# A hybrid decoder layer: every third weight piece with seven products instead of every fourth, and two of the four weight sums formed by accumulating transfers

## The chip, the core and the metric

The kernel runs on one core of one Trainium2 chip. The metric is device time in microseconds (us) of one execution; lower is better. TensorE (PE) does the matmuls, VectorE (DVE) and ScalarE (ACT) the elementwise work, SyncE (SP) issues most transfers, and GpSimd (POOL) does almost nothing before the change.

## The reference

One layer in float32, with 256 tokens, 16 meta tokens ahead of them and a width of 2048:

```python
h = RMSNorm(x)
[B, C, v | z, xBC, dt] = h @ W_in            # 2048 x 12320
yA = GroupRMSNorm(B * conv3(C * v))
yB = GroupRMSNorm(SSD(conv4(xBC), dt) * silu(z))
x = x + RMSNorm([yA | yB] @ W_out)           # 4096 x 2048
x = x + RMSNorm(relu(RMSNorm(x) @ W1)^2 @ W2)  # 2048 x 8192, 8192 x 2048
```

The change touches the two products whose result has the tokens on the partitions: `@ W_out` and `@ W2`.

## The kernel before

**Split products.** Every float32 operand is split into a high part in a shorter format (a cast on ScalarE) and a low part (a subtraction on VectorE). A product is then three matmuls: high by high, high by low, low by high. For a weight piece the parts are `wh` and `wl`, for activations `jh` and `jl`.

**Pieces.** All weights are read once, in pieces of 1 MB, in an order written out in the list `pieces`. `load(i)` gets a raw buffer (`raw`, 3 buffers), issues the transfer on SyncE's queue, and splits it into `wh` (3 buffers) and `wl` (2 and an extra one for every third piece). Program order is by hand: while piece i is multiplied, pieces up to i + 2 are loaded. The order on each engine's queue is laid out at compile time by a planner that simulates the engines with its own costs; each engine then runs its queue in order.

**The two stages.** `tok_stationary` does `W_out` (16 pieces a half) and `W2` (32 a half). The output's 2048 columns are done in two halves h of 1024. A piece holds 256 rows (two blocks of 128, index k) by 1024 columns (two blocks of 512, index nb); the tokens are two blocks of 128 (blk). A plain piece is 2 x 2 x 2 products of 128 x 128 by 128 x 512, added up in the four PSUM banks `four` (one for each blk and nb): 24 matmuls (L786 to L788).

**Seven-product pieces.** For the pieces listed in `fast`, the 2 x 2 x 2 block product is done with seven products in place of eight, in the manner of Strassen and Winograd: 21 matmuls (L817 to L819). It takes four mixed left blocks (`js`, split into `mix`, L772 to L777) and four mixed weight blocks `t` (L189 to L191), split into `th` and `tl`. Three products go to banks of `four`, four to the other banks, `shared`, which collect the terms that several results have in common. After the last such piece of a half, `spread_shared` (L829 to L834) forms from them one addend for each result, in SBUF. At the end of the half `leave` adds each addend to its bank (L848), squares and sums for the norm (L906), and multiplies by the gain (L853, L861). For the very last bank of the second half the addend is split by `shared_last` and added through TensorE with two matmuls by the identity (L842). The tiles `t`, `th` and `tl` have one buffer each.

**Order around it.** `add_up(i + 3)` asks for a seven-product piece's raw and forms its sums three pieces ahead, before `load` splits its `wh` and `wl`. `W_out` has `fast` pieces 7 and 10 in the first half, 2, 6 and 10 in the second; `W2` has every fourth from 4 to 28, and from 2 to 26. At the end of `W_out`, `residual` (L956) and transposes (L965) turn the first 128 tokens for the feed-forward stage. `dt_consts` (L477 on) copies constants from `cst_sb` at the start, where SyncE issues alternate between input rows and weights.

```python
halve(raw, wh, wl, slice(1, 2))                   # load(), a seven-product piece
nc.scalar.copy(wh[:, 0, :512], raw[:, 0, :512])
nc.vector.tensor_sub(wl[:, 0, :512], raw[:, 0, :512], wh[:, 0, :512])   # L206
```

Of the kernel before, what the change touches and what calls it, by code (L numbers as in the profile page):

```python
# [9 lines left out]
F32 = mybir.dt.float32  # L10
F32R = mybir.dt.float32r
# [35 lines left out]
def hymba_layer(ctx: ExitStack, tc: tile.TileContext, ht, x, meta, vec, cst, g1, g3,  # L47
# [131 lines left out]

    seven, sums = {}, {}  # L180

    def add_up(i):

        if i not in seven or i in sums:
            return
        raw = fetch(i, ("raw",))[0]
        rows_in(i, raw, slice(0, 2))
        t, th, tl = seven[i]()
        nc.vector.tensor_sub(t[:, 0:2], raw[:, :, 512:], raw[:, 0].rearrange("p (a n) -> p a n", a=2))  # L189
        nc.vector.tensor_sub(t[:, 2], raw[:, 1, 512:], t[:, 0])  # L190
        nc.vector.tensor_sub(t[:, 3], raw[:, 1, :512], t[:, 2])  # L191
        for half in (slice(0, 2), slice(2, 4)):
            halve(t, th, tl, half)
        sums[i] = (raw, th, tl)

    def load(i):
# [3 lines left out]
        if i in seven:  # L200
            add_up(i)
            raw, th, tl = sums[i]
            wh, wl = fetch(i, ("wh", "wl"))
            halve(raw, wh, wl, slice(1, 2))
# [6 lines left out]
        for k in range(0, nk, 1 if ff1 else nk // 2):  # L211
            if ff1:
                g = vcol(V_G2 + (i - base_ff1) % 4 * 4 + k)
                act(wh[:, k], raw[:, k], AF.Copy, scale=g)  # L214
                stt(wl[:, k], raw[:, k], g, wh[:, k].bitcast(F32), op0=ALU.mult, op1=ALU.subtract)  # L215
            else:
                halve(raw, wh, wl, slice(k, k + nk // 2))
# [9 lines left out]
    cst_sb = const.tile([P, NCST], F32, name="cst_sb")  # L227
# [69 lines left out]
    with ExitStack() as p1:  # L297
# [25 lines left out]
        def split_input(k):  # L323
# [9 lines left out]
            if k == 8:  # L333
                nc.sync.dma_start(vec_sb[:, V_GCN:], vec[:, V_GCN:])
                nc.sync.dma_start(cst_sb, cst)

        first = []

# [136 lines left out]
        def dt_consts():  # L475
            ts(vec_sb[:, V_CW:V_DSK], vec_sb[:, V_CW:V_DSK], 0.5, None, op0=ALU.mult)
            nc.vector.tensor_copy(nsel.rearrange("p i m -> p (i m)"), cst_sb[:, C_NS:C_NS + 384])  # L477
# [266 lines left out]
    def tok_stationary(base, korder, src, parity, dst, gain, ssq, r, tail, done, between, late=None, sixth=None,  # L744
# [12 lines left out]
        def prep(i):  # L757
# [10 lines left out]
            if base + i in seven:  # L768
# [3 lines left out]
                nc.vector.tensor_add(a[:, 0], a21, a22)  # L772
                nc.vector.tensor_sub(a[:, 1], a[:, 0], a11)
                nc.vector.tensor_sub(a[:, 2], a11, a21)
                nc.vector.tensor_sub(a[:, 3], a12, a[:, 1])
# [49 lines left out]
        def spread_shared(x, h):  # L825
# [7 lines left out]
            add(e12, e12, e22)  # L833
            add(e22, e21, e22)  # L834

        def shared_last(o):

            hi = jit.tile([P, 2, SEQ], F32R, tag="jh", name="sh").rearrange("p a b -> p (a b)")
            lo = jit.tile([P, 2, SEQ], F32R, tag="jl", name="sl").rearrange("p a b -> p (a b)")
            nc.scalar.copy(hi, part(1, 1, 1))  # L840
            nc.vector.tensor_sub(lo, part(1, 1, 1), hi)
            later(3, lambda: [mm(o, lhsT=idr, rhs=e, start=False, stop=False) for e in (hi, lo)])  # L842

        def leave(o, h, blk, nb):
            i = 2 * h + nb
            ns = slice(512 * i, 512 * (i + 1))
            if fast[h] and (h, blk, nb) != (1, 1, 1):
# [316 lines left out]
```

## Time and profile before

| | |
|---|---|
| median of 3 runs | 1514.04 us (1513.62 to 1514.47) |
| the profiled execution's own time | 1515.25 us |
| its span, first to last instruction | 1513.5 us |
| granted TensorE clock, mean | 0.995 |
| busy: PE, PEld, DVE, ACT, POOL | 1491.7, 1338.3, 1123.7, 839.8, 1.1 us |
| HBM read | 277.90 MB, 185 GB/s over the span |

The profile shows one execution. A row of a timeline is start, duration, engine, line, operation, output<-inputs, count; in square brackets stands how long the engine was idle before it and what it waited for. Rows of groups give the busy time, the mean duration of one in ns, and the idle time before. PEld is the loading of a matmul's stationary operand, which overlaps matmuls; a matmul's duration includes its pipeline, so its cost in a full queue is the distance from one start to the next. An elementwise operation's duration likewise overlaps its neighbours' by some 0.08 us.

### The profile page before, as it was taken

Reading aid. Unit: us, or ns where it says so; the run is one execution under the profiler, and the core shown is the slowest. Engines: PE = TensorE matmul, PEld = TensorE weight load, DVE = VectorE, ACT = ScalarE, POOL = GpSimd, SP = SyncE. Lnnn points to the kernel's source line nnn. Section 1 sums busy time; section 2 is a strip of 40 time slices with the busy share of each in tenths; the row PEclk is TensorE's granted clock in tenths of the full one; section 3 lists DMA queues with packets and bytes.
Section 4 is the critical chain, followed back from the end, with each engine's and each line's share of the span. In section 5 each row is a group of like instructions: output and inputs, shape, how many; then the busy total and the mean of one; then the engine's idle time right before and its main releaser. Section 6 shows DMA issues by size and latency. Waiting matters only on the chain.

```text
span 1513.5 us, 23117 instructions
## 1 busy us (share of the span) xinstructions
PE 1491.7 (99%) x9183; PEld 1338.3 (88%) x9183; DVE 1123.7 (74%) x1774; ACT 839.8 (55%) x1301; POOL 1.1 (0%) x8
## 2 busy tenths in 40 slices
PE   8999999999999999999999999999999999999997
PEld 8999899999999999988877888888888888888885
DVE  7698888667866776798878666566666788789875
ACT  6655555455545554555556656555556556566562
POOL 0000000000000000000000000000000000000000
PEclk9999999999999999999999999999999999999998
DMA  9665554556455656575653555565556565656652
GB/s 306 230 190 166 142 152 155 167 174 173 156 165 170 169 165 211 183 247 177 213 195 139 180 187 190 195 193 184 189 189 204 197 198 195 219 172 233 197 195 82
DMA packets 151677, 281.50 MB, mean 186 GB/s; under 512 B 8064, under 2 KB 59392, under 8 KB 150912
## 3 DMA queue, kind: packets, MB, share of 16 engines
q1 hardware_dynamic: 150848, 275.83, 56.8%
q10 hardware_dynamic: 720, 4.19, 0.7%
q8 instruction: 72, 1.18, 0.3%
q14 instruction: 37, 0.30, 0.1%
HBM read 277.90 MB, written 2.10 MB: 185 GB/s over the span
## 4 chain that ended last, share of the span: by engine, by line
PE 95%; DMA 2%; DVE 1%; ACT 1%; SPq 0%; issue 0%; DVEq 0%; ACTq 0%
PE mm L1083 15%; PE mm L643 11%; PE mm L642 10%; PE mm L641 10%; PE mm L787 9%; PE mm L788 9%; PE mm L786 9%; PE mm L1084 7%; PE mm L638 3%; PE mm L819 2%; PE mm L818 2%; PE mm L817 2%; DMA raw<-w_in 1%; PE aux L608 1%; PE mm L1001 1%; PE mm L999 0%
## 5 line engine op out<-in xcount | busy, mean ns | idle before, releaser
L175 DVE TENSOR_TENSOR wl<-raw,wh 128x1024 fp32r<-128x1024 f32 (+1 forms) x373 | 434.8, 1198 | 120.5 <-PE mm L643 56.0
L174 ACT CAST wh<-raw 128x1024 fp32r<-128x1024 f32 (+1 forms) x373 | 367.6, 1028 | 203.8 <-PE mm L642 120.4
L643 PE MATMUL mm<-XX,wl 128*128 128x256 f32 (+3 forms) x1536 | 426.8, 285 | 0.0
L641 PE MATMUL mm<-XX,wh 128*128 128x258 f32 (+3 forms) x1344 | 382.2, 288 | 5.7 <-ACT wh L174 5.7
L642 PE MATMUL mm<-XX,wh 128*128 128x258 f32 (+3 forms) x1344 | 379.1, 286 | 0.0
L1083 PE MATMUL mm<-h,wh 128*128 128x512 f32 x960 | 333.3, 394 | 0.0
L643 PEld LDWEIGHTS mm<-XX,wl 128*128 128x128 f32 x1536 | 286.1, 189 | 1.4 <-issue 0.2
L1084 PE MATMUL mm<-h,wl 128*128 128x256 f32 x960 | 265.7, 277 | 0.0
L641 PEld LDWEIGHTS mm<-XX,wh 128*128 128x128 f32 x1344 | 253.1, 190 | 8.1 <-ACT wh L174 5.7
L642 PEld LDWEIGHTS mm<-XX,wh 128*128 128x128 f32 x1344 | 252.5, 189 | 1.5 <-issue 0.7
L215 DVE SCALAR_TENSOR_TENSOR wl<-raw,vec_sb,wh 128x512 fp32r<-128x512 f32 x256 | 175.4, 747 | 100.7 <-ACT wh L214 100.7
L787 PE MATMUL mm<-wl,jh 128*128 128x512 f32 x616 | 239.9, 390 | 0.0
L788 PE MATMUL mm<-wh,jl 128*128 128x512 f32 x616 | 239.4, 390 | 0.0
L786 PE MATMUL mm<-wh,jh 128*128 128x512 f32 x616 | 235.8, 390 | 0.0
L1083 PEld LDWEIGHTS mm<-h,wh 128*128 128x128 f32 x960 | 180.0, 188 | 41.6
L214 ACT ACTIVATE wh<-raw,vec_sb 128x512 fp32r<-128x512 f32 x256 | 163.8, 712 | 89.1 <-PE mm L1083 50.7
L1084 PEld LDWEIGHTS mm<-h,wl 128*128 128x128 f32 x960 | 180.2, 188 | 0.3
L787 PEld LDWEIGHTS mm<-wl,jh 128*128 128x128 f32 x616 | 116.0, 188 | 24.1
L788 PEld LDWEIGHTS mm<-wh,jl 128*128 128x128 f32 x616 | 116.0, 188 | 23.9
L786 PEld LDWEIGHTS mm<-wh,jh 128*128 128x128 f32 x616 | 115.9, 188 | 23.9
L765 ACT CAST jh<-h 128x512 fp32r<-128x512 f32 x64 | 39.7, 620 | 107.0 <-PE mm L787 104.3
L766 DVE TENSOR_TENSOR jl<-h,jh 128x512 fp32r<-128x512 f32 x64 | 44.1, 689 | 41.3 <-ACT jh L765 39.1
(610 smaller groups left out, 1390.5 us busy)
## 6 DMA issues: line engine op xcount, KB each, us to landing
raw<-w_ff SPq DMA_DIRECT2D x128, 1024.0 KB, 5.1
raw<-w_in SPq DMA_DIRECT2D x60, 1024.0 KB, 5.2
raw<-w_out SPq DMA_DIRECT2D x32, 1024.0 KB, 5.1
raw<-w_in SPq DMA_DIRECT2D x80, 256.0 KB, 4.8
raw<-w_in SPq DMA_DIRECT2D x32, 512.0 KB, 4.1
xn<-x SPq DMA_DIRECT2D x2, 1024.0 KB, 5.2
xt<-x ACTq DMA_DIRECT2D x2, 1024.0 KB, 6.8
out<-fg SPq DMA_DIRECT2D x8, 256.0 KB, 2.2
```

What stands on the lines that cost most here:

```text
L174: nc.scalar.copy(wh[:, ks], raw[:, ks])
L175: nc.vector.tensor_sub(wl[:, ks], raw[:, ks], wh[:, ks])
L214: act(wh[:, k], raw[:, k], AF.Copy, scale=g)
L215: stt(wl[:, k], raw[:, k], g, wh[:, k].bitcast(F32), op0=ALU.mult, op1=ALU.subtract)
L641: mm(o[:, :n], lhsT=wh[:, k, fs], rhs=XH[kk][:, lo:], start=(kk == 0), stop=False)
L642: mm(o[:, :n], lhsT=wh[:, k, fs], rhs=XL[kk][:, lo:], start=False, stop=False)
L643: mm(o[:, :n], lhsT=wl[:, k, fs], rhs=XH[kk][:, lo:], start=False, stop=last)
L786: mm(o, lhsT=yh[:, k, bs], rhs=wh[:, k, ns], start=first, stop=False)
L787: mm(o, lhsT=yh[:, k, bs], rhs=wl[:, k, ns], start=False, stop=False)
L788: mm(o, lhsT=yl[:, k, bs], rhs=wh[:, k, ns], start=False, stop=last)
L1083: mm(o, lhsT=wh[:, k, fs], rhs=both, start=(kk == 0), stop=False)
L1084: mm(o[:, :SEQ], lhsT=wl[:, k, fs], rhs=both[:, :SEQ], start=False, stop=(kk == KD - 1))
```

## The change

- `fast` gets piece 13 in the first half of `W_out`, and every third piece in place of every fourth in `W2`: 4 to 28 and 2 to 26.
- `pair_up(i + 4)` asks for the raw of a seven-product piece four pieces ahead. ScalarE copies two of its blocks into `t[:, 0:2]`, and two transfers issued on GpSimd's queue add the two right-hand blocks (`raw[:, k, 512:]`, 256 KB each) onto them. `add_up(i + 3)` keeps the third and fourth sum on VectorE. `th` and `tl` are now formed in `load`, `tl` in one operation of 2048 elements.
- The signs of the sums change, as an accumulating transfer adds; the mixed left blocks and `spread_shared` follow.
- `shared_late` adds the addends of both banks with nb = 1 of the second half through TensorE, four matmuls with the identity in place of two; `leave` leaves out L848 for both.
- Plain pieces of `W_out` (from the third on) and of `W2` have their low part subtracted in one operation in place of two.
- The 384 columns of constants that `dt_consts` reads come by a transfer of their own into a scratch tile, and `cst_sb` is smaller by as much; the scratch for descriptors of GpSimd's transfers is 1024 in place of 256.

```diff
-    def add_up(i):
+    def pair_up(i):
         if i not in seven or i in sums:
             return
         raw = fetch(i, ("raw",))[0]
         rows_in(i, raw, slice(0, 2))
         t, th, tl = seven[i]()
-        nc.vector.tensor_sub(t[:, 0:2], raw[:, :, 512:], raw[:, 0].rearrange("p (a n) -> p a n", a=2))
-        nc.vector.tensor_sub(t[:, 2], raw[:, 1, 512:], t[:, 0])
-        nc.vector.tensor_sub(t[:, 3], raw[:, 1, :512], t[:, 2])
-        for half in (slice(0, 2), slice(2, 4)):
-            halve(t, th, tl, half)
-        sums[i] = (raw, th, tl)
+        nc.scalar.copy(t[:, 0:2], raw[:, 0].rearrange("p (a n) -> p a n", a=2))
+        for k in range(2):
+            nc.gpsimd.dma_start(t[:, k], raw[:, k, 512:], accum_op=ALU.add)
+        sums[i] = [raw, th, tl, t]
+
+    def add_up(i):
+        if i not in seven or len(sums[i]) == 3:
+            return
+        raw, _, _, t = sums[i]
+        nc.vector.tensor_add(t[:, 2], raw[:, 1, 512:], t[:, 0])
+        nc.vector.tensor_add(t[:, 3], raw[:, 1, :512], t[:, 2])
+        sums[i].pop()
+        sums[i, "t"] = t
...
         if i in seven:
+            pair_up(i)
             add_up(i)
             raw, th, tl = sums[i]
+            t = sums[i, "t"]
             wh, wl = fetch(i, ("wh", "wl"))
+            for half in (slice(0, 2), slice(2, 4)):
+                nc.scalar.copy(th[:, half], t[:, half])
+            nc.vector.tensor_sub(tl, t, th)
             halve(raw, wh, wl, slice(1, 2))
...
-            else:
+            elif i < base_out + 2:
                 halve(raw, wh, wl, slice(k, k + nk // 2))
+            else:
+                nc.scalar.copy(wh[:, k], raw[:, k])
+        if not ff1 and i >= base_out + 2:
+            nc.vector.tensor_sub(wl, raw, wh)
...
-    cst_sb = const.tile([P, NCST], F32, name="cst_sb")
+    cst_sb = const.tile([P, C_NS], F32, name="cst_sb")
...
-                nc.sync.dma_start(cst_sb, cst)
+                nc.sync.dma_start(cst_sb, cst[:, :C_NS])
+                nc.sync.dma_start(ns_sb, cst[:, C_NS:])
...
+        ns_sb = scratch("sq")[:, :NCST - C_NS]
...
-                nc.vector.tensor_add(a[:, 0], a21, a22)
+                nc.vector.tensor_sub(a[:, 0], a21, a22)
...
-                nc.vector.tensor_sub(a[:, 3], a12, a[:, 1])
+                nc.vector.tensor_add(a[:, 3], a12, a[:, 1])
...
-            add(e12, e12, e22)
-            add(e22, e21, e22)
+            nc.vector.tensor_sub(e12, e22, e12)
+            nc.vector.tensor_sub(e22, e22, e21)
-        def shared_last(o):
-            hi = jit.tile([P, 2, SEQ], F32R, tag="jh", name="sh").rearrange("p a b -> p (a b)")
-            lo = jit.tile([P, 2, SEQ], F32R, tag="jl", name="sl").rearrange("p a b -> p (a b)")
-            nc.scalar.copy(hi, part(1, 1, 1))
-            nc.vector.tensor_sub(lo, part(1, 1, 1), hi)
-            later(3, lambda: [mm(o, lhsT=idr, rhs=e, start=False, stop=False) for e in (hi, lo)])
+        def shared_late(four):
+            _, hi, lo = room()
+            for j, blk in ((0, 0), (1, 1)):
+                nc.scalar.copy(hi[:, j], part(1, blk, 1))
+                nc.vector.tensor_sub(lo[:, j], part(1, blk, 1), hi[:, j])
+                later(3 + j, lambda j=j, blk=blk: [mm(four[2 * blk + 1], lhsT=idr, rhs=e[:, j], start=False, stop=False)
+                                                  for e in (hi, lo)])
...
-            if fast[h] and (h, blk, nb) != (1, 1, 1):
+            if fast[h] and (h, nb) != (1, 1):
...
-                add_up(base + npc * h + i + 3)
+                pair_up(base + npc * h + i + 4)
+                if base + npc * h + i + 3 in sums:
+                    add_up(base + npc * h + i + 3)
...
-                   lambda blk: blk or residual(blk), between, late, first_gain, ((7, 10), (2, 6, 10)), mixp)
+                   lambda blk: blk or residual(blk), between, late, first_gain, ((7, 10, 13), (2, 6, 10)), mixp)
...
-                   fast=(range(4, 29, 4), range(2, 27, 4)), mixp=mixp, half_gain=g3_half)
+                   fast=(range(4, 29, 3), range(2, 27, 3)), mixp=mixp, half_gain=g3_half)
...
-    nc = bacc.Bacc("TRN2", target_bir_lowering=False, num_devices=1, dynamic_dma_scratch_size=256)
+    nc = bacc.Bacc("TRN2", target_bir_lowering=False, num_devices=1, dynamic_dma_scratch_size=1024)
```

More of the change, by code (lines that the diff above doesn't have):

```diff
@@ L215, in load @@
                 stt(wl[:, k], raw[:, k], g, wh[:, k].bitcast(F32), op0=ALU.mult, op1=ALU.subtract)
-            else:
-                halve(raw, wh, wl, slice(k, k + nk // 2))
+            elif i < base_out + 2:
+                halve(raw, wh, wl, slice(k, k + nk // 2))
+            else:
+                nc.scalar.copy(wh[:, k], raw[:, k])
+        if not ff1 and i >= base_out + 2:
+            nc.vector.tensor_sub(wl, raw, wh)
         parts[i] = (wh, wl)
@@ L476, in dt_consts @@
             ts(vec_sb[:, V_CW:V_DSK], vec_sb[:, V_CW:V_DSK], 0.5, None, op0=ALU.mult)
-            nc.vector.tensor_copy(nsel.rearrange("p i m -> p (i m)"), cst_sb[:, C_NS:C_NS + 384])
+            nc.vector.tensor_copy(nsel.rearrange("p i m -> p (i m)"), ns_sb)
             for i in range(6):
@@ L887, in tok_stationary @@
                 if fast[h] and h == 1 and i == fast[h][-1] + 2:
-                    shared_last(four[3])
+                    shared_late(four)
             for i in range(n, npc + (h == 0)):
```

## The prediction

> **What bounds the kernel now.** I read the page first (busy shares, chain), then who waited for whom, then windows and timelines of the stages that the change touches. First the page's engine row and everything that TensorE waited for; last the windows of two stretches (columns: length, busy time of PE, weight loads, VectorE, ScalarE, GpSimd, granted clock, DMA share, GB/s).
>
> ```profile
> PE 1491.7 (99%) x9183; PEld 1338.3 (88%) x9183; DVE 1123.7 (74%) x1774; ACT 839.8 (55%) x1301; POOL 1.1 (0%) x8
> ...
> PE mm L641 <- ACT wh L174: 5.7, 1, 5.7
> PE mm L965 <- DVE hres L956: 4.7, 1, 4.7
> PE aux L359 <- DVE dg L358: 0.6, 1, 0.6
> ...
> 1206.00:1227.00 21.00, 21.00 (x94) 17.38 (x94) 17.35 (x22) 12.06 (x15) 0.00 (x0) 1.00 0.61 199
> ...
> 1353.00:1374.00 21.00, 21.00 (x95) 17.38 (x93) 20.91 (x31) 14.49 (x18) 0.00 (x0) 1.00 0.63 202
> ```
>
> TensorE waits three times in the whole run: for the first weights, before the transposes at L965, and once for 0.6 us. In both stages that hold seven-product pieces it is full at granted clock 1.00, so there a matmul left out is worth its pitch, as long as nothing else becomes late. VectorE has 17% to spare in the second feed-forward stage, and next to none where that stage changes halves (20.91 of 21).
>
> **Matmuls.** The pitch comes from the first and last of the 21 matmuls of one seven-product piece; the counts from their line, and from the two that add the shared part at L842.
>
> ```profile
> 1185.18 0.39 PE L817 MATMUL mm<-wh,jh 128*128 128x512 f32 x1
> ...
> 1189.72 0.39 PE L819 MATMUL mm<-th,jl 128*128 128x512 f32 x1
> ...
> L817 PE MATMUL mm<-wh,jh x38: 389/389/389, 662.2 to 1470.8; 128*128 128x512 f32 x38
> ...
> L842 PE MATMUL mm<-sh,idr x2: 389/389/389, 783.3 to 1490.5; 128*128 128x512 f32 x2
> ```
>
> 20 steps in 4.54 us: 0.227 us a matmul. A plain piece issues 2 x 2 x 2 x 3 = 24, a seven-product piece 21. Two such (wh,jh) matmuls a piece and 38 of them make 19 pieces before. After, the second feed-forward stage has 9 + 9 in place of 7 + 7 and the output projection 3 + 3 in place of 2 + 3: 24. Five more pieces save 5 x 3 = 15 matmuls, 3.40 us. The shared part now enters two banks through TensorE at the end of each second half: 4 identity matmuls for 2, in two stages, 4 x 0.227 = +0.91 us. Both are certain, as TensorE has no hole at those places. Net -2.49 us.
>
> **VectorE and ScalarE.** Their costs per form, in the second feed-forward stage:
>
> ```profile
> L175 DVE TENSOR_TENSOR wl<-raw,wh 128x1024 fp32r<-128x1024 f32 x99 | 118.5, 1222 | 5.7 <-ACT wh L174 5.7
> L766 DVE TENSOR_TENSOR jl<-h,jh 128x512 fp32r<-128x512 f32 x56 | 38.6, 689 | 36.3 <-ACT jh L765 36.3
> ...
> L189 DVE TENSOR_TENSOR t<-raw 128x1024 f32<-128x1024 f32 x13 | 15.9, 1221 | 7.3 <-DMA raw<-w_ff 7.3
> L777 DVE TENSOR_TENSOR mix<-js,mix 128x512 fp32r<-128x512 f32 x13 | 8.9, 686 | 0.0
> ...
> L190 DVE TENSOR_TENSOR t<-raw,t 128x512 f32<-128x512 f32 x13 | 8.9, 685 | 0.0
> L775 DVE TENSOR_TENSOR js<-h,js 128x128 f32<-128x128 f32 x12 | 3.4, 287 | 0.0
> ...
> L174 ACT CAST wh<-raw 128x1024 fp32r<-128x1024 f32 x99 | 99.4, 1046 | 18.4 <-PE mm L819 18.1
> ```
>
> A 1024-element operation takes 1.22 us on VectorE, a 512-element one 0.69, two of 1024 back to back 2.36 (I use that for the new ones of 2048 too). A plain piece costs 2.36 + 0.69 = 3.05. A seven-product piece before costs 1.22 + 2 x 0.69 for t, 2.36 for tl, 1.91 for wl, 0.69 for jl, 4 x 0.29 + 0.69 for the mixed left side: 9.4; without the 1.22, 8.2. Four pieces before: 3 x 3.05 + 9.4 = 18.6 by these durations, 17.35 in the window since neighbours overlap (ratio 0.93). Three pieces after: (2 x 3.05 + 8.2) x 0.93 = 13.3 us in 69 x 0.227 = 15.66 us. The share goes from 83% to 85%: more sums, each cheaper by one operation, so VectorE doesn't become the bound on average. ScalarE gains one 1.05 us copy per seven-product piece; its 57% (12.06 of 21) goes to about 72%. Both costs lie beside TensorE and count zero while pieces are ready in time.
>
> **The two accumulating transfers** of 256 KB replace that 1.22 us subtraction, and nothing in the trace shows one. Nearest rows, issue to landing, with the 1 MB loads beside which they run:
>
> ```profile
> raw<-w_ff SPq DMA_DIRECT2D x128, 1024.0 KB, 5.1
> ...
> raw<-w_in SPq DMA_DIRECT2D x80, 256.0 KB, 4.8
> ...
> out<-fg SPq DMA_DIRECT2D x8, 256.0 KB, 2.2
> ...
> wdt<-w_in SPq DMA_DIRECT2D x1, 256.0 KB, 7.1
> ```
>
> So one takes 2.2 (source in SBUF, idle engines) to 7.1 us (busy engines); I take 4.8, the median of the 80 loads of that size into SBUF beside others, and add 0.4 for issuing the second behind the first. A = 5.2, from 2.6 to 7.5. In bytes it is 512 KB per three pieces beside 3 MB; the DMA share of 0.61 rises by a sixth to a third (the destination is read as well), to 0.8 at most. GpSimd's queue held nothing but 8 memsets, so nothing is queued behind them there. On VectorE the third and fourth sum wait for them, and behind these wait, in order, the splits of the plain pieces.
>
> By the Trainium skill's page "DMA: Bandwidth & Descriptors", section "Anatomy of one DMA", a transfer issued by GpSimd costs a fixed 2.0 us plus its bytes at 436 GB/s. An estimate by it is 2.6 us for 256 KB, 3 us for the pair, near my lower end. The sum would be the same, the rival below less likely; no row here shows such a transfer.
>
> **Where lateness could come in** is the raw buffers, three of 1 MB. The SyncE issues, the last reader of a seven-product piece's raw, and the ScalarE row that TensorE releases when the high-part buffer comes free:
>
> ```profile
> 1210.29 0.37 SPq L171 DMA_DIRECT2D raw<-w_ff  x1
> ...
> 1214.29 0.37 SPq L171 DMA_DIRECT2D raw<-w_ff  x1
> ...
> 1216.49 0.62 ACT L765 CAST jh<-h 128x512 fp32r<-128x512 f32 x1 [2.64 <-PE mm L787]
> ...
> 1220.81 0.68 DVE L206 TENSOR_TENSOR wl<-raw,wh 128x512 fp32r<-128x512 f32 x1
> ...
> 1221.52 0.37 SPq L171 DMA_DIRECT2D raw<-w_ff  x1
> ```
>
> Each load goes out when VectorE has let go of a buffer (L206 ends at 1221.49, the issue is at 1221.52). After, the raw of the next seven-product piece is asked for ahead of the plain piece before it, and reuses the buffer of the seven-product piece three earlier; the plain load stands behind it in SyncE's queue. From the release of that buffer to the next release: landing 5.1, ScalarE's copy 1.05, A, two sums 1.37, which is 7.5 + A, if wh and wl are split while t is still under way. If th, tl are put ahead of wl on both engines, add 2.0 + 2.36 + 1.83 = 6.2: 13.7 + A. The period is 15.66. In the first order this closes for any A below 8.1, so for all of my range, with 3 us left at A = 5.2. In the program th and tl stand first, but they can't start before t is there, and when the high-part buffer comes free wh can. With A = 5.2 and a release 8 us into the period, t is ready 8 + 7.5 + 5.2 = 20.7, or 5.0 into the next; the buffers come free at 4.8 (21 matmuls). So wh goes first or just alongside, and I cost the transfers at 0 on TensorE. Lateness eats first what is left: 3 us.
>
> **Rest.** At the end of the output projection the transposes wait (4.7 us) for this chain, with the last bank's add L848 and gain between:
>
> ```profile
> 790.59 0.69 DVE L848 TENSOR_TENSOR hres<-hres,mm 128x512 f32<-128x512 f32 x1 [0.25 <-PE mm L788]
> ...
> 791.91 0.19 ACT L906 ACTIVATION_READ_ACCUMULATOR junk<-hres 128x1 f32 x1
> ...
> 793.39 0.69 DVE L853 TENSOR_TENSOR hres<-hres,g1t 128x512 f32<-128x512 f32 x1 [0.18 <-ACT junk L906]
> ...
> 794.18 0.16 DVE L858 SCALAR_TENSOR_TENSOR rv<-ssq,rv 128x1 f32<-128x1 f32 x1
> ...
> 796.20 1.97 PE L965 MATMUL mm<-cst_sb,hres 128*128 128x128 f32 x8 [4.71 <-DVE hres L956]
> ...
> 11.38 0.33 SPq L335 DMA_DIRECT2D cst_sb<-cst  x1
> ...
> L831 DVE TENSOR_TENSOR fg<-fg,mm 128x512 f32<-128x512 f32 x2 | 1.4, 688 | 0.7 <-PE mm L819 0.7
> ...
> L829 ACT COPY fg<-mm 128x512 f32<-128x512 f32 x2 | 1.1, 575 | 0.0
> ```
>
> One L848 goes (its bank now arrives whole). VectorE is nearly gapless from 790.59 to 794.6, so at most its 0.61 us pitch comes off by that; the next add's own bank isn't finished earlier, so I take half, -0.3 (bounds 0 and -0.6). In the last stage the same add is long over before the end: 0. At the start one more issue on SyncE (0.33 us at L335, some 0.4 with its gap) delays the hidden loads; the chain there ends in the 0.6 us wait at L359, which could grow by 0.4. Bounds 0 and +0.4, taken 0. Splitting a plain piece's low part in one operation delays its first half by 1.2 us, hidden two pieces ahead of use. Moving the last sum of the first half of the output projection from piece 10 to 13 leaves one piece (5.4 us) to empty the shared banks with 2 copies and 2 adds (2 x 0.58 + 2 x 0.69 = 2.5 us), which is enough.
>
> **Sum**: 1515.25 (this execution, 1.75 above its span) - 2.49 - 0.3 = 1512.46. This execution stood 1.21 above the median of 1514.04; by that the forecast is 1511.2, 0.19% faster. 0.2% (3.0 us) is about what a measurement of this kernel tells from no change.
>
> **Rivals.**
>
> (a) Slower: t ahead of wl. If the order laid out at compile time takes the transfers for shorter than they are, th stands ahead of wh in ScalarE's queue and holds it, and the loop is 13.7 + A. It decides above A = 1.9. At A = 5.2 each of the 16 spans between seven-product pieces takes 3.2 us too long; each half of 8 first uses up about 5 us of lead: 2 x (26 - 5) = +42, 1553. At A = 2.6 it is 0.6 x 8 = 5 a half, all covered. Midway, +16: 1527. For it: program order, and VectorE has waited for landings here before (7.3 us at L189). Against: 3 us of play in the other order.
>
> (b) Single stalls where VectorE is full, above all at the change of halves:
>
> ```profile
> 1363.33 0.69 DVE L206 TENSOR_TENSOR wl<-raw,wh 128x512 fp32r<-128x512 f32 x1
> ...
> 1364.70 0.39 PE L817 MATMUL mm<-th,mix 128*128 128x512 f32 x1
> ```
>
> The piece is ready 0.7 us before its use. A later by 1.2 to 4 us than the subtraction costs 0.5 to 3 us there, and a little in the output projection: 1512 to 1515, within 0.2%. Against: this piece's raw is asked for one piece earlier than before.
>
> (c) Faster: L858 needs only the sum read at 791.91 to 792.10, but stands behind other work until 794.18. If the new order puts it right there, 2.0 us come off: 1509.5.
>
> (d) By the Trainium skill's page "SBUF — State Buffer", section "Who interferes with whom", VectorE with two SBUF inputs and a GpSimd instruction that reads SBUF shut each other out. Nothing here can show it. For the sum, as a mechanism of this kernel: were VectorE held for an issue (0.37 us, SyncE's row) twice in 15.66 us, its 85% would become 90%, no loss; it costs from 1.2 us an issue on. Chance 0.03, counted with (a).
>
> **Numbers.** Forecast 0.48 (1510.8 to 1511.6; a third of it beyond 0.2%), (a) and (d) 0.25, (b) 0.14, (c) 0.13. Faster 0.15 + 0.13 = 0.28, same 0.33 + 0.14 = 0.47, slower 0.25. The forecast's own range is 1510.5 to 1512; that for 8 in 10 is 1509.3 to 1524: of (a) it leaves out the upper two thirds.
>
> **What would show it.** 24 pieces at L817 and 8 identity matmuls; TensorE without waits from 1165 to the end but the known ones; landings of the accumulating transfers of 3 to 8 us; SyncE's issues in threes 15.7 us apart. Wrong, if TensorE waits for tl or wl, or if VectorE waits for the transfers over 3 us per three pieces.

## The result and the profile after

The changed kernel takes 1528.24 us (median; 1524.16 to 1532.58), the kernel before 1514.26 beside it: ratio 1.0094, 95% interval 1.0069 to 1.012. The change makes the kernel 0.9% slower; the forecast was 1511.2, its own range 1510.5 to 1512, and the range for 8 in 10 ended at 1524. The profiled execution after took 1524.16, the lowest of its four runs, so the 4 us from there to the median are in no profile. All line numbers below are those of the kernel named with the view; after the change the plain pieces' split is at L231/L233, the pair of transfers at L190, the third and fourth sum at L198/L199, their high and low part at L214/L215, the matmuls at L805 to L807 (plain) and L836 to L838 (seven products).

From the page of the changed kernel: the engines, the chain that ended last by line, and two issues with their median time to landing.

```profile
PE 1494.1 (98%) x9172; PEld 1336.6 (88%) x9172; DVE 1117.5 (73%) x1706; ACT 873.1 (57%) x1342; POOL 43.5 (3%) x56
...
PE mm L1105 15%; PE mm L662 11%; PE mm L661 10%; PE mm L660 10%; PE mm L1106 7%; PE mm L806 6%; PE mm L807 6%; PE mm L805 6%; DMA t<-raw 4%; PE mm L657 3%; PE mm L838 2%; PE mm L837 2%; PE mm L836 2%; DMA raw<-w_in 2%; DVE wl L233 1%
...
raw<-w_ff SPq DMA_DIRECT2D x128, 1024.0 KB, 5.5
...
t<-raw POOLq DMA_DIRECT2D x48, 256.0 KB, 6.6
```

TensorE issues 11 matmuls fewer, 9172 for 9183, which is the 15 less and 4 more of the prediction; yet it is busy 2.4 us longer, and some of them run at half clock (below). VectorE is less busy than before (73% for 74%), so it isn't short of time. New on the chain is a transfer, t<-raw.

What the engines waited for (in total, how often, longest); first all rows of TensorE above 1 us, then those that wait for the transfers.

```profile
PE mm L806 <- DVE wl L233: 5.7, 4, 4.6
PE mm L660 <- ACT wh L174: 5.6, 1, 5.6
PE mm L836 <- DVE y L310: 2.0, 1, 2.0
PE mm L836 <- ACT th L214: 1.7, 1, 1.7
PE mm L987 <- DVE hres L978: 1.6, 1, 1.6
...
ACT th L214 <- DMA t<-raw: 47.2, 17, 5.6
...
DVE t L198 <- DMA t<-raw: 33.4, 19, 5.8
```

Of the three waits before, that at the flips (the transposes at the end of the output projection; 4.7) is down to 1.6, and new ones have come for a plain piece's low part, wl L233, and for the sums' high part, th L214. VectorE and ScalarE stood 33 and 47 us in front of the transfers.

The largest new wait is at the change of halves. Timelines of GpSimd, VectorE and TensorE there (start, duration, what ended the idle time before):

```profile
1340.29 1.77 POOL L190 DMA_DIRECT2D t<-raw  x2 [15.65 <-DVE wl L175]
...
1342.80 0.68 DVE L785 TENSOR_TENSOR jl<-h,jh 128x512 fp32r<-128x512 f32 x1
1347.82 0.69 DVE L198 TENSOR_TENSOR t<-raw,t 128x512 f32<-128x512 f32 x1 [4.33 <-DMA t<-raw]
1348.43 2.28 DVE L233 TENSOR_TENSOR wl<-raw,wh 128x2048 fp32r<-128x2048 f32 x1
...
1345.32 0.84 PE L805 MATMUL mm<-wh,jh 128*128 128x512 f32 x3
1350.76 0.79 PE L806 MATMUL mm<-wl,jh 128*128 128x512 f32 x1 [4.60 <-DVE wl L233]
1351.36 0.63 PE L807 MATMUL mm<-wh,jl 128*128 128x512 f32 x1
```

The first of the two transfers is issued at 1340.29. VectorE is done with everything else at 1343.5, takes the third sum, L198, and stands in front of it 4.33 us until the transfer lands. Behind it in its queue is the split of a plain piece, whose high part ScalarE had ready at 1342.9 and which TensorE needs from 1346.2 on: a piece that isn't part of the new sums at all. TensorE waits 4.60 us.

The windows around it (length, busy time of PE, weight loads, VectorE, ScalarE, GpSimd, then granted clock, DMA share, GB/s), and that of the middle of the stage:

```profile
1343.00:1346.00 3.00, 3.00 (x14) 2.27 (x13) 0.48 (x1) 0.62 (x1) 0.00 (x0) 1.00 0.93 266
1346.00:1349.00 3.00, 0.17 (x1) 0.00 (x0) 1.19 (x2) 0.54 (x1) 0.00 (x0) 1.00 1.04 286
1349.00:1352.00 3.00, 1.24 (x3) 1.05 (x4) 3.00 (x4) 1.98 (x3) 0.00 (x0) 0.50 0.42 109
1352.00:1355.00 3.00, 3.00 (x8) 2.32 (x8) 3.00 (x4) 0.62 (x1) 0.00 (x0) 0.50 0.91 318
1355.00:1358.00 3.00, 3.00 (x12) 2.42 (x12) 1.71 (x6) 0.00 (x0) 0.00 (x0) 0.86 0.79 244
...
1170.00:1320.00 150.00, 150.00 (x664) 124.20 (x663) 123.85 (x139) 100.73 (x125) 14.07 (x16) 1.00 0.80 234
```

While the pair is under way the transfer engines are full (1.04), with a 1 MB weight load and the gain's 512 KB beside it. Once TensorE starts again its granted clock is 0.50 until about 1355.8, 5 us of work at half speed, so the 4.6 us wait costs some 7 (an estimate: 4.6 and half of 5). In the stage's middle the DMA share is 0.80, the prediction's upper estimate, and TensorE doesn't wait there: the loss is made in a few places. By stage, the profiled pair differ by 8.9 us of span: +0.9 in the output projection, +9.3 in the second feed-forward stage, -1.4 after the last matmul, +0.1 at the start.

### The profile page after: what moved, and what is told of

Its sections match the earlier page's. It is cut to its first block, busy times and chain, and to the rows that moved or that the text cites. A ratio compares the mean times of both kernels' runs of the same rounds, so it can differ in the third digit from the quotient of the medians.

```text
span 1522.4 us, 23225 instructions
## 1 busy us (share of the span) xinstructions
PE 1494.1 (98%) x9172; PEld 1336.6 (88%) x9172; DVE 1117.5 (73%) x1706; ACT 873.1 (57%) x1342; POOL 43.5 (3%) x56
## 4 chain that ended last, share of the span: by engine, by line
PE 84%; DMA 7%; DVE 4%; ACT 2%; issue 2%; SPq 0%; POOL 0%; DVEq 0%; ACTq 0%
PE mm L1105 15%; PE mm L662 11%; PE mm L661 10%; PE mm L660 10%; PE mm L1106 7%; PE mm L806 6%; PE mm L807 6%; PE mm L805 6%; DMA t<-raw 4%; PE mm L657 3%; PE mm L838 2%; PE mm L837 2%; PE mm L836 2%; DMA raw<-w_in 2%; DVE wl L233 1%
## 5 line engine op out<-in xcount | busy, mean ns | idle before, releaser
L175 DVE TENSOR_TENSOR wl<-raw,wh 128x1024 fp32r<-128x1024 f32 (+1 forms) x228 | 262.1, 1182 | 106.4 <-PE mm L662 56.9
L174 ACT CAST wh<-raw 128x1024 fp32r<-128x1024 f32 (+1 forms) x228 | 223.2, 1017 | 182.1 <-PE mm L661 119.0
L806 PE MATMUL mm<-wl,jh 128*128 128x512 f32 x576 | 226.1, 393 | 5.7 <-DVE wl L233 5.7
L807 PE MATMUL mm<-wh,jl 128*128 128x512 f32 x576 | 224.9, 392 | 0.0
L805 PE MATMUL mm<-wh,jh 128*128 128x512 f32 x576 | 219.2, 391 | 0.5 <-ACT wh L231 0.5
L233 DVE TENSOR_TENSOR wl<-raw,wh 128x2048 fp32r<-128x2048 f32 x70 | 160.1, 2288 | 30.0 <-ACT wh L231 27.4
L231 ACT CAST wh<-raw 128x1024 fp32r<-128x1024 f32 x140 | 139.6, 1045 | 43.9 <-DMA raw<-w_ff 14.7
L806 PEld LDWEIGHTS mm<-wl,jh 128*128 128x128 f32 x576 | 109.0, 189 | 30.6 <-DVE wl L233 8.0
L805 PEld LDWEIGHTS mm<-wh,jh 128*128 128x128 f32 x576 | 108.7, 189 | 23.6 <-ACT wh L231 1.0
L807 PEld LDWEIGHTS mm<-wh,jl 128*128 128x128 f32 x576 | 109.1, 189 | 22.5
```

The costliest lines, as they stand in the source:

```text
L174: nc.scalar.copy(wh[:, ks], raw[:, ks])
L175: nc.vector.tensor_sub(wl[:, ks], raw[:, ks], wh[:, ks])
L233: nc.vector.tensor_sub(wl, raw, wh)
L805: mm(o, lhsT=yh[:, k, bs], rhs=wh[:, k, ns], start=first, stop=False)
L806: mm(o, lhsT=yh[:, k, bs], rhs=wl[:, k, ns], start=False, stop=False)
L807: mm(o, lhsT=yl[:, k, bs], rhs=wh[:, k, ns], start=False, stop=last)
```

## The experiments

Three theories. T: the accumulating transfers are late, and what stands behind them in order is what TensorE misses. D: the density of seven-product pieces is too much for VectorE. Rival (a) of the prediction: the sums' parts stand ahead of the weights' parts, and the loop of buffers doesn't close.

**Without the transfers.** The transfers and the copy ahead of them go, and the first two sums are one VectorE instruction.

```
-        nc.scalar.copy(t[:, 0:2], raw[:, 0]...)
-        for k in range(2):
-            nc.gpsimd.dma_start(t[:, k], raw[:, k, 512:], accum_op=ALU.add)
...
+        nc.vector.tensor_add(t[:, 0:2], raw[:, :, 512:], raw[:, 0]...)
```

> The changed kernel without its accumulating transfers: all four weight sums on VectorE, as before the change, with everything else of the change kept (every third piece, raw asked for four pieces ahead, late shared part). Theory T (the transfers land late, about 9 us after the first issue where 5.2 was taken, and the work queued behind them stalls TensorE): TensorE's waits of 4.6 us at the change of halves, 2 to 3 us around 1400 and 2.8 us around 660 to 670 go, and the time is 1509 to 1512. Rival D (every third piece is too dense for VectorE, or the early raw of the sum pieces delays the plain ones): VectorE has 1.2 us more per three pieces, so the waits stay or grow, 1522 to 1535.

1511.77 (ratio to before 0.9984, 0.9975 to 0.9992). The transfers, with ScalarE's copy ahead of each pair, cost 16.5 us; no run separates the copies (1.05 us each) from the transfers. D falls as the main cause.

**The pieces of before, with the transfers.** `fast=(range(4, 29, 4), range(2, 27, 4))` and `(7, 10), (2, 6, 10)`.

> The changed kernel with the lists of pieces of before (every fourth; 19 seven-product pieces), so the transfers, the early raw and the late shared part without the denser pieces. Theory T: the change of halves still has its 0.5 MB gain load, a raw load and two transfers at once, so TensorE still waits some 3 to 6 us there and 2 to 3 us at the first two pieces of the output projection: 1517 to 1523. Rival D: with VectorE back at its old load the waits go: 1509 to 1514.

1524.17 (1.0064, 1.0051 to 1.0077), 4.1 us less, though 15 more matmuls cost 3.4. So density has a share. By an estimate, without the transfers this version would stand at 1511.8 + 3.4 = 1515.2, so they cost some 9 us here in place of 16.5. But the loop of 15.66 us a period isn't the whole of it: with a period a third longer the waits are still there (TensorE waits 7.5 us for L233, in six places), although the median pair now takes 5.92 us from its first issue to its second landing, not far above the prediction's 5.2. TensorE's three longest waits for L233 (2.95 at 764.8, 1.32 at 1366.3, 2.37 at 1390.3) each come just behind a late pair (9.22, 12.66 and 9.42 us), with VectorE standing 5.3 to 6.9 us in front of the third sum: single late landings are enough.

**Weights' parts first in the program.** The lines of `th`, `tl` moved behind those of `wh`, `wl` in `load`.

> The changed kernel with one order turned round in a seven-product piece: wh and wl are split ahead of th and tl in the program. Theory T with my rival (a) of the prediction (th stands ahead of wh and holds ScalarE while t is under way, loop 13.7 + A): the raw buffer is let go some 6 us earlier and most waits in the feed-forward stage go: 1512 to 1518. If the place of th in the order is not what costs, but VectorE standing at the third sum for the landing (4.3 us idle there ahead of the 4.6 us wait), little changes: 1522 to 1532.

1527.45 (1.0082, 1.0069 to 1.0095): no change. The planner lays out the engines' order by its own estimates, and moved little for this edit. The next two edits met the same: the third and fourth sum called later in the program (only in `load`), and the gain's half loaded at piece 12 in place of the half's start.

> The changed kernel with the third and fourth sum formed when the piece is loaded, one piece later in program order. Theory T (VectorE stands at the third sum for a landing that comes 9 us after the issue, with the splits of plain pieces behind it): the sums stand behind a plain piece's split, VectorE's waits for the transfers (33 us in all in the changed kernel) fall below 10 us and TensorE's wait at the change of halves falls from 4.6 to below 2 us: 1514 to 1520. If what counts is when th and tl are ready, this makes them later: 1526 to 1534.

1527.15 (1.0082, 1.006 to 1.0104), with VectorE still in front of L198 ahead of a plain split, 4.27 us at the change of halves.

> The changed kernel with the 0.5 MB gain load of the last stage asked for in the middle of each half (piece 12) and no longer at its start. If the wait of 4.6 us at the change of halves comes from three streams at once (weights, gain, accumulating pair) it goes, and with it the slower clock behind it: 6 to 8 us less, 1520 to 1523. If the pair and the weights alone are enough, it stays: 1526 to 1530.

1526.49 (1.0081, 1.0069 to 1.0093), but the gain's load was still issued at 1347, so this told nothing of that load's share. What was tested in these three is the order of the program, not the order on the engines.

**The order on VectorE, forced.** The two sums are held behind the split of the plain piece before them, and are called only in `load`, as in the version of 1527.15.

```
+        with tc.issue_after(plain_wl[i - 1].ins) if i - 1 in plain_wl else nullcontext():
             nc.vector.tensor_add(t[:, 2], raw[:, 1, 512:], t[:, 0])
             nc.vector.tensor_add(t[:, 3], raw[:, 1, :512], t[:, 2])
...
-            nc.vector.tensor_sub(wl, raw, wh)
+            plain_wl[i] = nc.vector.tensor_sub(wl, raw, wh)
```

> The changed kernel, with the third and fourth sum of a piece held behind the split of the plain piece before it on VectorE, so that VectorE doesn't stand in front of a transfer while a split that TensorE needs sooner is queued behind. Transfers, pieces and sizes stay. Theory (the time goes because VectorE, in order, waits for the transfer ahead of the plain split): the 4.6 us wait of TensorE at the change of halves goes, and with it the stretch at half clock, 3.4 us: 1528.2 falls to 1519 to 1522. Rival (what counts is how late the transfers land, whoever waits): TensorE's waits stay 6 us or more in FF2, at the seven-product pieces or at the copies of ScalarE, and the time is 1525 to 1529.

1517.9 (1.002, 1.0011 to 1.0028), 10.3 us less with the same transfers, and a little below T's 1519 to 1522. ScalarE still stands 45.2 us in front of the transfers, where it stood 47.2, so a shorter wait of ScalarE isn't what brings the 10.3 us. VectorE at the change of halves, in this kernel (the sum is L199, the split L234):

```profile
1344.48 2.29 DVE L234 TENSOR_TENSOR wl<-raw,wh 128x2048 fp32r<-128x2048 f32 x1
...
1347.60 2.29 DVE L234 TENSOR_TENSOR wl<-raw,wh 128x2048 fp32r<-128x2048 f32 x1
1349.81 0.68 DVE L199 TENSOR_TENSOR t<-raw,t 128x512 f32<-128x512 f32 x1
```

The splits go first and the sum finds its transfer landed (no idle time in front of it). Of the 4.60 us wait there 1.38 is left, and the half clock behind it is gone; against that, the flips' wait has grown to 3.6, with 6.8 us at half clock behind it.

**The pair by itself.** First, six transfers late in the second feed-forward stage of the kernel without transfers.

```
+            for k in range(2):
+                nc.gpsimd.dma_start(t_[:, k], hres[:, 1, 512 * k:512 * (k + 1)], accum_op=ALU.add)
+            for k in range(2):
+                nc.gpsimd.dma_start(t_[:, 2 + k], t_[:, 1 - k])
+            for k in range(2):
+                nc.sync.dma_start(t_[:, k], t_[:, 3 - k])
```

> The changed kernel with all sums on VectorE, and, after the last weight load, six extra transfers of 256 KB between SBUF tiles whose result nothing uses: a pair that accumulates and a pair that copies, both issued by GpSimd, then a pair that copies issued by SyncE, each pair after the one before. It asks whether a pair of accumulating transfers is slow by itself or because weight loads share the DMA engines. If sharing is the cause: the accumulating pair lands about 4 us after its first issue (first 2.5 to 3.4, second about the same), like the copies. If accumulating is slow by itself: 6.6 us or more for its second transfer with nothing else moving, against about 3 us for the copies.

1512.83 (one run). They went out at 1467, beside the last two weight loads, so they weren't alone: 5.1 and 8.1 us for the accumulating ones, 4.9 and 5.5 for plain copies from the same engine. Put where nothing is left to load, with the last left-hand side as the source:

> The kernel with all four sums on VectorE, with six transfers of 256 KB added in the tail, where the last weights have been loaded and the transfer engines would stand idle: two accumulating transfers from GpSimd, then two plain copies within SBUF from GpSimd, then two plain copies from SyncE, each pair waiting for the one before. It measures the disputed cost by itself; its output is that of the kernel without them. If an accumulating transfer is slow of itself, the pair takes 7 us or more here too and the plain copies from GpSimd clearly less (5 us or less). If it is slow because it shares the transfer engines with the weight loads, the pair takes 3 to 5.5 us here, near the plain copies from the same engine. Prediction on record: 5.2 us, from 2.6 to 7.5. Time of the kernel 1509 to 1513, as without the transfers.

1511.72 (one run). Issues from 1480 to 1495 in this kernel, median us to landing:

```profile
t<-jh POOLq DMA_DIRECT2D x2, 256.0 KB, 3.9
t<-t POOLq DMA_DIRECT2D x2, 256.0 KB, 2.3
t<-t SPq DMA_DIRECT2D x2, 256.0 KB, 2.3
```

Alone, an accumulating transfer takes 3.5 and 4.3 us, the pair from the first issue (1484.18) to the second landing (1489.19) 5.0; a plain copy takes 2.3 from either engine. Accumulating is dearer by 1.2 us or more, but it isn't what makes 9.

**The next weight load held back.** A transfer of two elements a partition on SyncE, which reads both results, stands between the pair and the next load.

```
+        sink = left.tile([P, 2], F32, tag="sink", name="sink")
+        seen.append(nc.sync.dma_start(sink, t[:, 0:2, 0]))
...
+            with tc.issue_after(seen[-1].ins) if seen else nullcontext():
                 nc.sync.dma_start(raw[:, ks, lo:hi], src[:, ks])
```

> The changed kernel with the next weight load held on SyncE until the pair of accumulating transfers has landed (a transfer of two elements a partition that reads their result stands ahead of it). Nothing is left out. If the pair is slow because its second transfer shares the engines with the load issued 0.5 to 1.2 us behind it (it lands about 1.2 us after that load): the pair takes 4.5 to 6 us instead of 7 to 10, as in the idle tail (5.0). If it is slow by itself, or through loads issued ahead of it: 7 us or more stay. The time is not the question: each load that is held starts some 6 us later, so 1520 to 1550.

Time to landing of the accumulating transfers' line, min/median/max, in the changed kernel:

```profile
DMA to landing us min/median/max: 3.3/6.6/10.7
```

and in this one, with the largest group of TensorE's waits:

```profile
DMA to landing us min/median/max: 3.3/4.1/5.9
...
PE mm L808 <- ACT wh L234: 33.2, 21, 2.3
```

Worked out for all 24 pairs from their issue and landing times, a pair takes 9.07 us (median; 4.97 to 11.25) in the changed kernel and 4.85 (4.82 to 6.41) here. So 4.2 of the 9.1 us come from the weight loads beside it. The changed kernel's window from 1201 to 1202 shows one such case (issues, median us to landing):

```profile
raw<-w_ff SPq DMA_DIRECT2D x1, 1024.0 KB, 6.6
t<-raw POOLq DMA_DIRECT2D x2, 256.0 KB, 6.4
```

The 6.4 is the middle of the two. The first transfer, issued at 1200.86, lands after 3.67. The load goes out at 1201.94, 0.55 behind the second transfer, and lands at 1208.55; the second transfer lands behind it, at 1210.47, 9.07 us after its own issue (this pair: 9.61 from its first issue). The load itself takes 6.6, where the median of the weight loads before is 5.1. By the Trainium skill's page "DMA: Bandwidth & Descriptors", section "Issuing engines are not separate DMA queues", transfers run on the same DMA engines and interleave whoever issued them; these rows agree. The time, 1664.2 (1.099, 1.0976 to 1.1004), is far above what I expected, 1520 to 1550: the loads, each some 6 us later, are then late in every period, and TensorE waits in some 75 places. Holding loads back is no remedy.

**The other parts of the change, alone.** Late shared banks (`shared_late`, and the condition in `leave`) in the kernel before, all else as before:

> The kernel before with one part of the change alone: the addends of both banks with nb = 1 of the second halves go in through TensorE (4 identity matmuls for 2 in each stage), and two L848 adds go. By the terms of the prediction: +0.91 us for four matmuls, -0.3 at the transposes: 1514.9. By the trace of the changed kernel the part is worth more: the wait before the transposes was 1.6 in place of 4.7 us, and the stretch from the last matmul to the end 9.8 in place of 11.2 us: together with +0.91 that makes 1509.5 to 1511.

1506.88 (0.9951, 0.9939 to 0.9963), 7.6 us less than the kernel before beside it, and below both figures expected. VectorE at the flips in the kernel before, then VectorE and TensorE there in this kernel (the add is L849, the gain L854, the residual L957, the transposes L966):

```profile
789.65 0.69 DVE L848 TENSOR_TENSOR hres<-hres,mm 128x512 f32<-128x512 f32 x1 [4.29 <-PE mm L788]
...
787.12 0.69 DVE L849 TENSOR_TENSOR hres<-hres,mm 128x512 f32<-128x512 f32 x1 [3.25 <-PE mm L788]
788.60 0.69 DVE L854 TENSOR_TENSOR hres<-hres,g1t 128x512 f32<-128x512 f32 x1 [0.79 <-ACT junk L907]
...
791.77 2.75 DVE L957 SCALAR_TENSOR_TENSOR hres<-hres,rr,xt 128x512 f32<-128x512 f32 x4
...
792.68 0.40 PE L788 MATMUL mm<-wh,jl 128*128 128x512 f32 x1
792.91 1.04 PE L966 MATMUL mm<-cst_sb,hres 128*128 128x128 f32 x8
```

The first block's add comes at 787.12, where before the first of three adds, close to one another, came at 789.65; the chain behind it is far enough while TensorE still has matmuls of the second block, so the transposes follow without a gap, and at full clock (8 in 1.04 us, before 1.97). The whole wait of 4.71 is gone, with the half clock behind it.

Then every third piece in the second feed-forward stage on top of that, sums on VectorE as before:

> The kernel before with the late shared part (1506.9 us) and every third piece in the second feed-forward stage, sums on VectorE three pieces ahead as before the change; the output projection keeps its lists. Four more pieces save 12 matmuls, 2.7 us. If VectorE has room for them: 1503.8 to 1505. If the change of halves, where VectorE was full, now stalls (1.7 us in the changed kernel without transfers): 1505.5 to 1508.

1504.15 (0.9932, 0.992 to 0.9944), 2.73 less: 4 pieces x 3 x 0.227 = 2.72. So close a match is luck: in the two profiles the stage, from its first matmul to its last, is 2.2 us shorter. And piece 13 of the output projection:

> The kernel before, with the late shared banks and every third piece in FF2 (1504.15), and in addition piece 13 of the first half of the output projection as a seven-product piece. Its sums are all on VectorE. By the matmuls alone: 3 x 0.227 = 0.7 less, 1503.5. Rival: the added piece brings back the wait at the flips (3.4 us with sums on VectorE and 10-13 pieces, and a stretch at half clock behind it): 1508 to 1511, which would place the 7.6 us between that version and the changed kernel without transfers there.

1504.47 (0.9924, 0.9911 to 0.9938): neither the 0.7 us nor a wait can be told. And, without that piece, the low part of a plain piece in one instruction:

```
-                halve(raw, wh, wl, slice(k, k + nk // 2))
+                nc.scalar.copy(wh[:, k], raw[:, k])
+        if not ff1 and i >= base_out + 2:
+            nc.vector.tensor_sub(wl, raw, wh)
```

> The kernel before, with the late shared banks and every third piece in FF2 (1504.15), and the low part of a plain piece formed by one VectorE instruction of 2048 elements instead of two of 1024, as in the changed kernel. If the single split costs nothing (2.28 us against two of 1.22): 1504. If the later first half of the low part holds TensorE at the flips, as with the changed kernel: 1506 to 1510.

1509.22 (0.996, 0.9947 to 0.9972): 5.1 us dearer by nothing else. What TensorE waited for in this kernel, and one of the places on VectorE and TensorE:

```profile
PE mm L791 <- DVE wl L221: 2.2, 3, 1.5
PE mm L970 <- DVE hres L961: 2.0, 1, 2.0
...
1293.26 1.23 DVE L189 TENSOR_TENSOR t<-raw 128x1024 f32<-128x1024 f32 x1 [3.33 <-DMA raw<-w_ff]
1294.40 2.29 DVE L221 TENSOR_TENSOR wl<-raw,wh 128x2048 fp32r<-128x2048 f32 x1
...
1296.74 0.50 PE L791 MATMUL mm<-wl,jh 128*128 128x512 f32 x1 [1.47 <-DVE wl L221]
```

VectorE stood 3.33 us in front of a weight load for the first sum; the plain split behind it then came out whole at 1296.7, where the first of two halves would have been out 1.1 us sooner. The flips' wait is back too, 2.0 us.

**The single split out of the changed kernel**, without and with the transfers.

> The changed kernel without the transfers (all four sums on VectorE, 1511.8) and with the low-part split in two halves. By the cost of the single split alone: 1511.8 - 5.1 = 1506.7, which leaves 2 us to the one-piece low part of the sums and the order of the rest. If the single split is all that separates it from the version of before with late shared banks and the same pieces (1504.5): 1504 to 1505.

1504.29 (0.9933, 0.9921 to 0.9944). All that this kernel's TensorE waited for, and its engines:

```profile
PE mm L654 <- ACT wh L174: 5.4, 1, 5.4
PE mm L654 <- ACT sz L719: 0.4, 1, 0.4
...
PE 1486.6 (99%) x9172; PEld 1334.2 (89%) x9172; DVE 1149.5 (77%) x1800; ACT 850.8 (57%) x1318; POOL 1.1 (0%) x8
```

The matmuls of the changed kernel, VectorE at 77% with every sum on it, and no wait at all behind the start.

> The changed kernel with its low-part split of a plain piece in two halves again, as before the change; transfers and all else stay. If the costs of the single split (5.1 us, alone) and of the transfers add: 1528.2 - 5.1 = 1523. If they are one lateness, in which the transfers' 9 us decide: no change, 1526 to 1529. If the single split is what makes the transfers' wait reach TensorE: 1508 to 1516.

1524.77 (1.0071, 1.0044 to 1.0097), runs from 1518.53 to 1535.47. The median is 3.5 us below the changed kernel, but the two intervals overlap, and 1523, what adding the costs gives, lies inside this one. So this run doesn't tell whether the single split and the transfers add or are in part one lateness. Last, both undone: the sums held behind the plain split, as above, and that split in two halves, with the transfers kept.

> The changed kernel with both undone: the third and fourth sum held behind the plain split on VectorE (alone 1517.9) and that split in two halves. If the costs add: 1517.9 - 5.1 = 1513, still above the 1504 to 1507 of the versions without transfers. If the transfers cost nothing once VectorE doesn't stand in front of them: 1504 to 1507. If ScalarE's wait for them at the high part of the sums is what is left: 1512 to 1518.

1514.21 (1.0, 0.9991 to 1.0008), 3.7 less than with the order alone. What is left of the transfers' cost, 9.9 us over the version without them, in the timelines of GpSimd, VectorE and TensorE (this execution took 1517.03, 2.8 above the median of its eleven):

```profile
1377.11 1.77 POOL L190 DMA_DIRECT2D t<-raw  x2 [18.20 <-ACT t L188]
...
1379.43 0.69 DVE L793 TENSOR_TENSOR mix<-js,mix 128x512 fp32r<-128x512 f32 x1
1385.37 0.69 DVE L199 TENSOR_TENSOR t<-raw,t 128x512 f32<-128x512 f32 x1 [5.25 <-DMA t<-raw]
1385.98 1.29 DVE L782 TENSOR_TENSOR jl<-h,jh 128x512 fp32r<-128x512 f32 x2
...
1386.72 0.50 PE L835 MATMUL mm<-wh,jl 128*128 128x512 f32 x1 [2.72 <-DVE jl L782]
```

VectorE stands in front of the same sum, 5.25 us; now it is the low part of the left-hand side, jl, that is queued behind it, and TensorE waits 2.72 us for that. Holding the sum behind one kind of work makes the next kind late.

The parts, one on top of the other:

| version | us | step |
|---|---|---|
| before | 1514.26 | |
| + late shared banks | 1506.88 | -7.4 |
| + every third piece in the second feed-forward stage | 1504.15 | -2.7 |
| + piece 13 in the output projection | 1504.47 | not resolved |
| + the rest of the change but the next two | 1504.29 | not resolved |
| + low part of a piece in one instruction | 1511.77 | +7.5 |
| + the accumulating transfers: the change | 1528.24 | +16.5 |

The kernel before stood at 1514.24 to 1514.81 in these comparisons, so half a microsecond means nothing. Three versions without the two last steps lie at 1504.2 to 1504.5, faster than both kernels.

## Why the prediction was wrong

**Failed: "I cost the transfers at 0 on TensorE".** They cost 16.5 us. Two links of that step broke. The term A, 5.2 us with 2.6 to 7.5, is 9.07 in place and 4.85 with the next load held back: I took it from rows of transfers that ran beside others but not from one issued together with a 1 MB load. The prediction's own condition, "closes for any A below 8.1", is then broken. But the loop isn't where most of the time went: at a period a third longer some 9 of the 16.5 us stayed (the estimate above), and the middle of the stage runs without waits. There the order that the loop rests on, "if wh and wl are split while t is still under way", held: in the changed kernel ScalarE has wh at 1205.44 and th at 1210.57. The link that broke is what stands behind the two sums: I named it ("the splits of the plain pieces") and gave it no price, as if that work were done first. VectorE takes its queue in order, the compile-time order had the sum in front, and the wait went to a piece that had nothing to do with the transfer. Forcing that one order took back 10.3 of the 16.5 us. The row that I showed for the release of "the high-part buffer" is that of the left-hand side's jh, not of a weight's wh, so it showed nothing of when wh can go. Of the two signs of being wrong one came: TensorE waits 5.7 us for wl. VectorE's waits for the transfers, 33.4 us for 24 pairs, stay on average below the 3 us a pair that I had set.

**Failed: the single split "hidden two pieces ahead of use", 0.** It costs 5.1 us alone and 7.5 in the changed kernel without transfers. The cover that I named, two pieces of lead, isn't there where VectorE has just waited for a load.

**Mis-sized: the flip chain, -0.3.** The stretch from the output projection's start to the second feed-forward stage shrank by 6.9 us, 4.7 of it the wait and the rest mostly the half clock behind it. I kept the order of the last matmuls fixed ("the next add's own bank isn't finished earlier") and took off one add. In the new order the add of the first block starts 2.5 us earlier. The tail, put at 0, gave 2.1 us with the late banks alone and 1.4 in the changed kernel.

**Right: the matmuls.** 15 less, 4 more; 2.73 us by the medians, 2.2 by the stage in the profiles, for 2.72 where four pieces were added alone, and the identity matmuls' 0.45 a stage stands in the second feed-forward stage of the late-banks version (339.34 us from its start to the last matmul, 338.89 before). The start cost +0.1 us, within 0 to 0.4. VectorE didn't become the bound.

**The rivals.** (a) named the cause, an order laid out for transfers shorter than they are, and its middle price, 1527, is near the result, which is luck: by its own formula a transfer midway, A = 3.9, costs 2 x (8 x 1.94 - 5) = 21 us and not 16, so 1532, and the runs don't show that loop. It put the order on ScalarE, and the price on a loop that falls behind by 3.2 us a period. The order that the runs show to matter is VectorE's, and the price comes in single waits. ScalarE stood in front of th 47 us in all; the forced order took 10.3 us off the time and left 45 of these 47, but no run took them alone away, so ScalarE's share of the rest stays open. (b) had the kind and the place, single waits above all at the change of halves, and there 4.6 us for 0.5 to 3: it left out that other, unrelated work stands behind the late sum, and the half clock. (c) came true only in the sense that the chain at the flips got shorter, for another reason. (d) had no run of its own, but the changed kernel's trace shows no sign of VectorE being held: 17 of its 2048-element splits, with two inputs each, run while GpSimd is busy with an issue, and take 2.29 us like the 49 others. In all, the gains came out larger than I had them, 10 us, and the two parts that I costed at zero took 24.

**What stays open.** Whether the two costs overlap (by the medians the transfers cost 16.5 on top of the single split, 20.5 without it) can't be told, as the runs of these two versions with transfers scatter by 8 and 17 us. Nor was it taken apart which of the 10 us left in the last version is VectorE's and which is ScalarE's, its copies included. That the second transfer is late through the loads issued behind it is shown by holding them; which of the shared resources it waits for isn't.

## What to carry to other kernels

An operation moved to another engine is not free where a third engine, in order, waits for its result: ask what is queued behind the waiting instruction, and force the order or count that work as late by the whole landing time. Price a transfer from rows of transfers issued beside the same loads, since here the same pair took 4.9 us with the next load held back and 9.1 beside it. Try a change's parts one at a time: here two parts gained 10 us and two others lost 24, and the sum alone would have had all four thrown away.

## What the runs showed of the hardware

A wait of TensorE can cost more than its length. Windows of the kernel before at the flips, after its wait of 4.71 us:

```profile
795.00:801.00 6.00, 4.80 (x17) 4.12 (x18) 4.35 (x8) 1.41 (x3) 0.00 (x0) 0.50 0.00 0
```

and of the single-split version, after its wait of 2.02 us (792.00 to 794.02):

```profile
785.00:795.00 10.00, 7.97 (x38) 6.06 (x37) 5.47 (x16) 2.62 (x8) 0.00 (x0) 1.00 0.33 107
795.00:800.00 5.00, 5.00 (x30) 4.20 (x28) 4.97 (x12) 4.12 (x8) 0.00 (x0) 1.00 0.01 2
```

Over all these profiles the half-clock stretches behind a single wait were 3.4 or 6.8 us long, and the wait's length alone didn't say which: 1.64 us at the flips brought 3.4 in two versions and nothing in three, 2.02 brought 3.4 in the changed kernel and nothing here, 3.4 at the flips brought nothing, 3.4 or 6.8 in three versions, 4.6 and 4.7 brought 6.8, and 5.0 in one version 3.4. The Trainium skill's page "TensorE: Matmul & The Clock Gate", section "Part 1: The HAM clock gate", has the clock set by how busy TensorE was in windows of about 3.4 us that run on their own; the lengths and the scatter agree with that. The longest stretch of work that ran at half clock behind one wait was some 6 us (6.8, of which 0.9 lay in the wait), so by an estimate from these profiles a wait can cost up to 3 us more than its length.

An accumulating transfer of 256 KB within SBUF took 3.3 us at the least, a plain one 2.3, and GpSimd was busy 0.86 to 1.25 us with the issue of each. The fit of the page "DMA: Bandwidth & Descriptors" of the Trainium skill, section "Anatomy of one DMA", gives an estimate of 2.6, which lies between the two.
